# Moving the second half of a gate projection behind the last input projection block, with the attention stage's loads, value split and first maxima beside it

## The chip, the core and the metric

The kernel runs on one core of one Trainium2 chip. A core has five engines that run side by side, each through a queue of its own in a fixed order: TensorE (PE, matrix products, with weight loads shown apart as PEld), VectorE (DVE), ScalarE (ACT), GpSimd (POOL) and SyncE (SP), which here issues most of the transfers between the large memory and the core's own. The metric is device time in microseconds (us), the median of several executions.

## The reference, cut to what matters

One layer of a backbone over 2048 latent tokens and 256 context tokens, width 1024: a modulated norm, one input projection, a softmax attention group and a gated delta-rule group side by side, an output projection, then a gated MLP.

```
q_a, k_a, v_a, qkv_d, z_d, a_f, a_b, b_f, b_b = jnp.split(h @ w_in, offs, axis=-1)
...
o_attn = block_attention(ql, jnp.concatenate([kc, kl], axis=1), jnp.concatenate([vc, vl], axis=1))
o_attn = rms_norm(o_attn.astype(h.dtype), attn_out_g)
...
qd, kd, vd = gdn_inputs(qkv_d, conv_qkv_w, True)
...
o_gdn = gated_rms(ol_f + flip(ol_b), z_d, gdn_norm_g)
lat_out = jnp.concatenate([o_attn, o_gdn], axis=-1) @ w_out
```

`z_d` is the gate: 512 columns of the input projection, put through SiLU and multiplied into the delta rule's normalised output. The attention has 8 query heads on 2 key heads of 64 columns, over 18 chunks of 128 keys (2 of context, 16 latent). The delta rule has 4 heads of 128 columns and runs over the same 18 chunks in both directions.

## The kernel before, in words

Products are done with operands split into a high and a low part, so that a product is three matmuls. The kernel goes through these stages, each on all tokens:

1. `front`: modulation, first norm, keys and values of the attention (stored to `ksc`, `vsc`). The normed input stays on the core in `hl`, four chunks of 512 tokens in two parts.
2. Attention queries (stored to `qsc`), two halves of 256 columns over 16 token tiles.
3. The gate, also two halves of 256 columns over 16 token tiles (the loop over `hf` and `tt` around L950 to L972). A tile is 24 matmuls (`tokproj`, L585 to L587), SiLU on ScalarE (L963), a scaling on GpSimd (L964), a maximum on VectorE (L967, into `zmx`) and a store by SyncE (L969, to `zsc`). The second half's weights are loaded and split by `load_w` (L576, L577). `decay_setup`, a long list of small steps for the delta rule, is put into the first half at its third tile.
4. Twelve input projection blocks for the delta rule (matmuls L546 to L548, output `pg`): four each for queries, keys and values. For each block and chunk: copy out (`u`, L1076), a convolution of three steps on VectorE (`y`, L1048, L1050), SiLU (L1051), transposes on PE (`pt`, L987), scaling (`kd`, L995, L998) and a store to `gsc` (L1000). `load_g` loads and splits a block's weights. From the fifth block on, the context chunk (`hc`) comes first in each block. The second modulation's pieces (`wm`, `wacc`, `mps2`) lie between.
5. The second norm's scales (`hm` to `oscl`, L1099 to L1128): maxima over `aff2`, `mod2`, the output gain and `zmx`, spread over the partitions through two small products on PE.
6. Attention and delta rule together. Both are written as lists of planned instructions (`Plan`), which a list scheduler orders by estimated costs, buffer rings and the weights of their tracks; the order is then issued as it is. All of them show the line L422, so they are told apart by tile names. The stage begins with clearing tiles (`rows`, `qx`, `kx`, L1161 to L1164), the loads of queries, keys and values by GpSimd (`q`, `qx`, `kh`, `kx`, `vraw`), the row maxima of the first query group (`tops`: products `sm`, maxima `mx`, then `top`, `tp` and a row of `qx`), the value split (`values`: `vm`, `vst`) and the delta rule's start values (`y`, twelve copies of `i16` on ScalarE).

   In the loop over 32 groups (16 query tiles by 2 key heads), the scores `sc` of two key chunks go through the exponential to `p`, are split into `hp` and `lp`, and are multiplied with the values into `ops`; the next group's maxima run between. The delta rule has 18 steps in each direction; each loads `tT`, `tk` and `rows`, inverts a triangular matrix (`py`, `pa`, `y`, `t`) and advances a state.
7. Output projection, second norm, MLP (`po`, `ua`, `ub`, `uc`, `pdn`).

Outside the planned stages the framework's own scheduler orders instructions by the place in the program and by estimated readiness; a later instruction may be put ahead of an earlier one that waits. On-chip room is taken from pools on a left and a right stack; a tile waits until the tiles that had its room are done with.

Of the kernel before, what the change touches and what calls it, by code (L numbers as in the profile page):

```python
# [10 lines left out]
F32 = mybir.dt.float32  # L11
# [9 lines left out]
P = 128  # L21
# [9 lines left out]
HA = 8  # L31
# [163 lines left out]
class Plan:  # L195
# [5 lines left out]
    def __init__(self, tc, *psum):  # L201
        self.tc, self.psum, self.ops, self.rings, self.open = tc, psum, [], {}, None
        self.track, self.spent, self.gate, self.patience, self.rate, self.fixed = None, {}, None, {}, 2.4, (65, 65, 0, 50, 42)
# [9 lines left out]
    def wrap(self, tile_, shape, dtype):  # L213
        return Lazy(Root(None, None, None, tile_), shape, dtype)

# [53 lines left out]
    def add(self, eng, fn, name, kw):  # L269
# [170 lines left out]
def kernel(  # L440
# [511 lines left out]

    with tc.tile_pool(name="zp", bufs=2, reuse_waits="tile") as zp_:
        for hf in range(2):
            for tt in range(NTT):
                if (hf, tt) == (0, 2):
                    decay_setup()
                n_ = f"z{hf}_{tt}"
                if (hf, tt) == (1, 10):
                    wg = load_g(0)  # L960
                ps = tokproj(direct, of_chunk(tt), ws, 256, n_)
                zt = zp_.tile([P, 256], F32, tag="zt", name=f"zt_{n_}")
                S.activation(out=zt, in_=ps[:, :256], func=AF.Silu)  # L963
                G.tensor_tensor(out=zt.rearrange("p (h d) -> p h d", d=P),  # L964
                                in0=zt.rearrange("p (h d) -> p h d", d=P),
                                in1=rows[:, R_GN:R_GN + P].unsqueeze(1).broadcast_to([P, 2, P]), op=ALU.mult)
                V.tensor_reduce(out=zmx[:, 16 * hf + tt:16 * hf + tt + 1], in_=zt, axis=AX, op=ALU.max,  # L967
                                apply_absolute_value=True)
                SY.dma_start(out=zsc[tt, :, 256 * hf:256 * hf + 256], in_=zt)  # L969
            if hf == 0:  # L970
                ws = load_w(direct, wiz[1], "z1")
    pq.close()  # L972


    with ExitStack() as pg:
        hcp = pg.enter_context(tc.tile_pool(name="hcp", bufs=1, side="right", reuse_waits="tile"))
        hc = hcp.tile([P, 2, KT, TC], F32R, name="hc")
# [87 lines left out]
        for blk in range(NG):  # L1065
            ws = wg if blk == 0 else load_g(blk)
            if blk == 2:
                SY.dma_start(out=hc.bitcast(F32), in_=hcd)
# [1381 lines left out]
```

## Time and profile before

| | us |
|---|---|
| median of 3 runs | 3199.56 (3194.95 to 3201.15) |
| the profiled execution | 3198.06 |
| its span, first to last instruction | 3196.3 |
| PE busy in the span | 3053.4 (96%) |
| VectorE, ScalarE, GpSimd busy | 2385.7, 1769.9, 1531.0 |

Stages by the trace: gate matmuls from 271.2 to 370.8 (the second half from 324.5), input projection blocks from 370.8 to 712.4, attention and delta rule from about 726 to 1740, then the rest. A row of the profile gives an engine's busy time, the number of instructions, and what ended the idle time before them; matmuls overlap each other, so a matmul's own duration is longer than the distance to the next one. PEclk is the share of full clock that PE was granted.

### The profile page before, as it was taken

To read this page: it belongs to the slowest core of one execution; us is meant where nothing else is said; L and a number is where in the kernel's file an instruction comes from. 1 tells how busy PE (TensorE), PEld (TensorE's weight loads), DVE (VectorE), ACT (ScalarE), POOL (GpSimd) and SP (SyncE) were. 2 spreads that over 40 slices of the span, in tenths; PEclk is the share of its full clock that TensorE was granted. 3 is DMA by queue.
4 is the path that set the end of the run, shared out by engine and by line. 5 is a ranking of instruction groups with operands and counts; after the bars stand their busy time and mean duration, and the time that the engine had idled before them with its cause. 6 is when DMAs were issued, how large, how long until landed. Compare 5 with 4: busy or idle time off the path is not lost.

```text
span 3196.3 us, 62950 instructions
## 1 busy us (share of the span) xinstructions
PE 3053.4 (96%) x25298; PEld 1958.4 (61%) x25298; DVE 2385.7 (75%) x3669; ACT 1769.9 (55%) x2876; POOL 1531.0 (48%) x1241
## 2 busy tenths in 40 slices
PE   6889999997999999999998999999999999999998
PEld 3789978874667777777776454444444444444445
DVE  4766487887777777788885779877777777976676
ACT  4534134345777777776776546545555455544332
POOL 4786365555887776776777434323332223000000
PEclk8899999997999999999998899999999999999999
DMA  6222334663112222233332575322222222696696
GB/s 245 82 79 83 112 120 125 174 172 94 46 41 75 67 82 87 87 117 109 102 104 100 205 258 193 125 93 99 96 98 97 94 98 77 204 311 204 218 308 221
DMA packets 287333, 423.63 MB, mean 133 GB/s; under 512 B 22984, under 2 KB 166952, under 8 KB 285744
## 3 DMA queue, kind: packets, MB, share of 16 engines
q1 hardware_dynamic: 285088, 414.19, 39.2%
q0 software_dynamic: 1952, 5.42, 0.6%
q8 instruction: 198, 3.24, 0.4%
q14 instruction: 95, 0.78, 0.1%
HBM read 284.15 MB, written 135.81 MB: 131 GB/s over the span
## 4 chain that ended last, share of the span: by engine, by line
PE 76%; DVE 9%; POOL 6%; DMA 3%; issue 3%; ACT 3%; SPq 0%; POOLq 0%; DVEq 0%; ACTq 0%
PE pdn L422 12%; PE ub L422 10%; PE sc L422 7%; PE uc L422 7%; PE ua L422 6%; PE ops L422 6%; PE po L422 6%; PE sm L422 3%; PE pa L422 2%; PE pg L547 1%; PE pg L546 1%; PE pg L548 1%; PE pw L422 1%; DVE mx L422 1%; PE pm L422 1%
## 5 line engine op out<-in xcount | busy, mean ns | idle before, releaser
L422 POOL TENSOR_TENSOR lp<-p,hp 128x1024 f16<-128x1024 f32 x288 | 620.0, 2160 | 208.5 <-DVE hp L422 83.4
L422 PEld LDWEIGHTS <-ws_u 128*128 128x128 f16 x3696 | 360.7, 98 | 434.3 <-issue 9.1
L422 DVE TENSOR_REDUCE mx<-sm 128x2 f32<-128x1024 f32 (+1 forms) x320 | 356.3, 1113 | 94.7 <-PE sm L422 91.5
L422 PE MATMUL pdn<-hid,wd 128*128 128x512 f16 (+1 forms) x1980 | 400.8, 365 | 0.0
L422 ACT ACTIVATE p<-sc 128x1024 f32<-128x1024 f32 x288 | 295.2, 1025 | 127.5 <-PE sc L422 123.8
L422 PEld LDWEIGHTS <-wd 128*128 128x128 f16 x1980 | 193.8, 98 | 204.7
L422 DVE SCALAR_TENSOR_TENSOR cv<-xa,ufw,cv 128x1025 f32<-128x1025 f32 (+1 forms) x176 | 251.3, 1480 | 49.9 <-ACT cv L422 49.8
L422 POOL TENSOR_TENSOR ws_u<-raw_u,ws_u 128x512 f16<-128x512 f32 x110 | 174.4, 1597 | 139.8 <-ACT ws_u L422 120.5
L422 PE MATMUL sc<-q,kh 128*128 128x512 f16 x576 | 220.6, 383 | 6.3 <-ACT p L422 5.9
L422 PE MATMUL sc<-qx,kx 128*128 128x512 f16 x576 | 220.4, 383 | 0.0
L422 POOL TENSOR_TENSOR nrc_f<-nrc_f,mhalf 128x8 f32<-128x8 f32 x3 | 5.5, 1837 | 423.7 <-DVE nrc_f L422 423.7
L422 ACT CAST hp<-p 128x1024 f16<-128x1024 f32 x192 | 201.0, 1047 | 3.7
L422 PE MATMUL ops<-vst,hp 128*128 128x65 f16 (+1 forms) x4608 | 192.3, 194 | 1.3 <-ACT hp L422 1.1
L422 PE MATMUL ua<-blk_a,ws_u 128*128 128x512 f16 x792 | 181.4, 379 | 0.0
L422 PEld LDWEIGHTS <-hp 128*128 128x128 f16 x4608 | 165.3, 98 | 21.0 <-issue 6.9
L422 PE MATMUL po<-ol,ws_o 128*128 128x512 f16 x768 | 175.0, 385 | 0.1
L546 PE MATMUL pg<-hl,ws_g 128*128 128x512 f32 x384 | 152.8, 398 | 0.0
L422 POOL TENSOR_TENSOR usg<-usg,mhalf 128x3 f32<-128x3 f32 x22 | 20.5, 933 | 276.1 <-DVE usg L422 276.1
L548 PE MATMUL pg<-hl,ws_g 128*128 128x512 f32 x384 | 152.3, 397 | 0.0
L547 PE MATMUL pg<-hl,ws_g 128*128 128x512 f32 x384 | 151.7, 395 | 0.0
L422 ACT CAST t<-pa 128x512 f16<-128x512 f32 x216 | 124.6, 583 | 43.1 <-PE pa L422 39.3
L422 PE MATMUL sm<-kh,q 64*128 64x512 f16 (+1 forms) x320 | 118.8, 371 | 18.4 <-DVE mx L422 18.1
(704 smaller groups left out, 7787.0 us busy)
## 6 DMA issues: line engine op xcount, KB each, us to landing
rd<-in_wd SPq DMA_DIRECT2D x70, 512.0 KB
hid<-hidc SPq DMA_DIRECT2D x70, 512.0 KB
raw_u<-in_wu SPq DMA_DIRECT2D x44, 512.0 KB
tk<-gsc SPq DMA_DIRECT2D x34, 512.0 KB
tT<-gsc SPq DMA_DIRECT2D x66, 256.0 KB
hidc<-cv SPq DMA_DIRECT2D x22, 768.0 KB
wm<-in_wm SPq DMA_DIRECT2D x64, 256.0 KB
gsc<-kd SPq DMA_DIRECT2D x64, 256.0 KB
```

Source lines behind the costliest of these rows:

```text
L422: fn(**{k: v.get() if isinstance(v, Lazy) else v for k, v in kw.items()})
L546: PE.matmul(out=ps, lhsT=hi_l(k), rhs=hi_r(k), start=st, stop=False)
L547: PE.matmul(out=ps, lhsT=hi_l(k), rhs=lo_r(k), start=False, stop=False)
L548: PE.matmul(out=ps, lhsT=lo_l(k), rhs=hi_r(k), start=False, stop=en)
```

## The change

The second half of the gate projection no longer follows the first. Its weights are loaded within the last block into tiles that held the context input (`hc` becomes four tiles of a ring, `zw` follows in it, and the attention's `p` tiles after that), split by ScalarE and GpSimd. Its 16 tiles run behind the last block, and between them, at the tiles named in `todo`, stand the attention stage's loads and clearings (`loads`, tile 0), the value split (`values`, tile 4) and the row maxima of the first two query groups (`first_tops`, tiles 6 and 10), now outside the plan, with single-bank products and one maximum for each. The value split multiplies by the scale while it converts and subtracts. The attention's planned part starts with the scores; the maxima of groups 0 and 1 are dropped from it. The second norm's scales become planned instructions behind the plan's instruction at which the ninth group begins, on a track of low weight. The delta rule's start values are copied by VectorE outside the plan, its first loads are issued by SyncE as all others are, without waiting for the keys' issue, and the buffer `at` is claimed one instruction earlier.

```
+    def claim(self, t):
+
+        r, o = t.root, self.ops[-1]
+        o.allocs.append(r)
+        r.turn, r.first = r.ring.made.get(o.track, 0), o.idx
+        r.ring.made[o.track] = r.turn + 1
+        r.ops.add(o.idx)
...
+        if self.after is not None:
+            op.behind.add(self.after)
...
+    def gate_tile(hf, tt, ws, pool, shape, tag):
+        n_ = f"z{hf}_{tt}"
+        ps = tokproj(direct, of_chunk(tt), ws, 256, n_)
+        zt = pool.tile(shape, F32, tag=tag, name=f"zt_{n_}", bufs=2)[:, 0:256]
+        S.activation(out=zt, in_=ps[:, :256], func=AF.Silu)
...
+        SY.dma_start(out=zsc[tt, :, 256 * hf:256 * hf + 256], in_=zt)
...
-        for hf in range(2):
-            for tt in range(NTT):
...
-            if hf == 0:
-                ws = load_w(direct, wiz[1], "z1")
+        for tt in range(NTT):
+            if tt == 2:
+                decay_setup()
+            if tt == 10:
+                wg = load_g(0)
+            gate_tile(0, tt, ws, zp_, [P, 256], "zt")
...
+                if (blk, c) == (NG - 1, 0):
+                    zw = []
+                    for i, t in enumerate(four_tiles("zw")):
+                        raw = rp.tile([P, 2, 256], F32, tag="raw", name=f"raw_z1{i}", bufs=3)
+                        SY.dma_start(out=raw, in_=wiz[1][:, 2 * i:2 * i + 2, :])
+                        S.copy(out=t[:, 0], in_=raw)
+                        G.tensor_tensor(out=t[:, 1], in0=raw, in1=t[:, 0].bitcast(F32), op=ALU.subtract)
+                        zw += [t[:, :, 0, :], t[:, :, 1, :]]
...
+    def loads():
+        for a in range(0, NCK, 6):
+            s = ksc[a:a + 6].rearrange("c p f t -> p c f t")
+            G.dma_start(out=kh_t[0:64, a:a + 6], in_=s[0:64])
+            G.dma_start(out=kh_t[64:128, a:a + 6], in_=s[0:64])
+        G.dma_start(out=vraw, in_=vsc.rearrange("c p x -> p c x"))
+        G.dma_start(out=q0_t, in_=qsc[0])
+        G.dma_start(out=qx_t[0][64:128], in_=qsc[0][0:64])
+        for t in qx_t:
+            G.memset(t[0:64], 0.0)
+        G.memset(kx_t[0:64], ROWV)
...
+    def values():
...
+        for g in range(KV):
+            x = vraw[:, :, g * HD:(g + 1) * HD]
+            S.activation(out=vst_t[:, :, g, 0:HD], in_=x, func=AF.Copy, scale=vi[:, g:g + 1])
+            V.scalar_tensor_tensor(out=vst_t[:, :, g, HD + 1:2 * HD + 1], in0=x, scalar=vi[:, g:g + 1],
+                                   in1=vst_t[:, :, g, 0:HD], op0=ALU.mult, op1=ALU.subtract)
...
+    def first_tops(g):
...
+        for h in range(0, GR, 2):
+            for j in range(5):
...
+                sm = [pst.tile([P, 512], F32, tag="pb", name=f"sm{g}_{h}_{j}_{i}") for i in range(2)]
...
+                for i in range(2):
+                    V.tensor_reduce(out=mx[:, h + i, j:j + 1], in_=sm[i][:, 0:w], axis=AX, op=ALU.max)
...
+    todo = {0: loads, 4: values, 6: lambda: first_tops(0), 10: lambda: first_tops(1)}
+    for tt in range(NTT):
+        if tt in todo:
+            todo[tt]()
+        gate_tile(1, tt, zw, ak, [P, 512], "oacc")
+    p1.close()
...
+    for d in range(2):
+        G.memset(rows_t[d], 0.0)
+        for t in ys_t[d]:
+            V.tensor_copy(out=t, in_=i16)
...
-        for _ in tops(0, 0, *q_now):
-            pass
-        values()
...
+            if n == 8:
+                marks.append(len(plan.ops) - 1)
...
-                pr = plan.tile(ap, [P, 2, 512], F32, "p", f"p_{nm}_{c0}", RINGS["p"])
+                pr = plan.tile(hcp, [P, 2, 512], F32, "hc", f"p_{nm}_{c0}", 4)
...
-            q = SY if step else G
-            plan.gate = None if step else loaded[0]
+            q = SY
...
+    plan.track, plan.after = "m", marks[0]
+    second_scales(plan)
+    plan.after = None
```

`second_scales` holds the same instructions as stage 5 above, written for the plan; `gate_tile` holds those of stage 3.

More of the change, by code (lines that the diff above doesn't have):

```diff
@@ new lines @@
+    ak = pa.enter_context(tc.tile_pool(name="ak", bufs=1, side="right", reuse_waits="tile"))
+    VW, GR = 130, HA // KV
+    kh_t = ak.tile([P, NCK, KV, P], F16, name="kh")
+    vraw = ak.tile([P, NCK, KV * HD], F32, name="vraw")
+    vst_t = ak.tile([P, NCK, KV, VW], F16, name="vst")
+    q0_t = ak.tile([P, HA, P], F16, name="q0")
+    qx_t = [ak.tile([P, HA, P], F16, name=f"qx{i}") for i in range(2)]
+    kx_t = ak.tile([P, NCK, KV, P], F16, name="kx")
+    shift_t = ak.tile([P, 1], F32, name="shift")
@@ L1133 @@
+    vtop_t = ak.tile([P, KV], F32, name="vtop")
     pc = ExitStack()
@@ new lines @@
+    todo = {0: loads, 4: values, 6: lambda: first_tops(0), 10: lambda: first_tops(1)}
[4 more added lines that the diff above has]
+    p1.close()
+    p2 = ExitStack()
+    gy = p2.enter_context(tc.tile_pool(name="gy", bufs=1, reuse_waits="tile"))
+    rows_t = [gy.tile([P, HG, 3, P], BF16, name=f"rows{d}") for d in range(2)]
+    ys_t = [[gy.tile([P, 512], F16, name=f"y{d}{l}") for l in range(1, 7)] for d in range(2)]
@@ L1188, in load_q @@
             qx = qxs[qb % 2]
[L1189 to L1191 removed]
+            SY.dma_start(out=qt, in_=qsc[qb])
+            SY.dma_start(out=qx[64:128], in_=qsc[qb][0:64])
             return qt, qx
[L1195 to L1201 removed]
@@ L1202, in attention @@
-        loaded.append(len(plan.ops) - 1)
-        for a in range(0, NCK, 6):
-            G.dma_start(out=kx[64:128, a:a + 6], in_=ksc[a:a + 6].rearrange("c p f t -> p c f t")[64:128])
-        shift = plan.tile(ak, [P, 1], F32, "shift", "shift", 1)
-        V.scalar_tensor_tensor(out=shift, in0=gm[:, 0:1], scalar=9.0 * SC / 1024, in1=gm[:, 1:2], op0=ALU.mult, op1=ALU.mult)
-        V.tensor_scalar(out=shift, in0=shift, scalar1=PSLACK * SC, scalar2=-1.0 / ROWV, op0=ALU.min, op1=ALU.mult)
-        V.tensor_scalar(out=shift, in0=shift, scalar1=PSHIFT * SC / ROWV, scalar2=None, op0=ALU.add)
@@ L1242, in tops @@
+        q_now = plan.wrap(q0_t, [P, HA, P], F16), qxs[0]
+        kh, kx = (plan.wrap(t, [P, NCK, KV, P], F16) for t in (kh_t, kx_t))
+        shift = plan.wrap(shift_t, [P, 1], F32)
+        vst = plan.wrap(vst_t, [P, NCK, KV, VW], F16)
+        vtop = plan.wrap(vtop_t, [P, KV], F32)
         def tops(qb, g, qt, qx):
@@ L1353, in delta @@
         s0 = None
-        ys = [None]
-        for l in range(1, 7):
-            y = plan.tile(gh, [P, 512], F16, f"y{d}{l}", f"y{d}{l}", 1)
-            S.copy(out=y, in_=i16)
-            ys.append(y)
+        ys = [None] + [plan.wrap(t, [P, 512], F16) for t in ys_t[d]]
         lvm = [None] + [lv16[:, P + 64 * (6 * d + l):P + 64 * (6 * d + l + 1)].bitcast(U16) for l in range(6)]
@@ L1382, in delta @@
             q.dma_start(out=rws[0:12], in_=rsc[d, ck].rearrange("h r s t -> r h (s t)"))
-            plan.gate = None
             if lat and not first:
@@ L1503, in delta @@
                 at = f32t("at")
+                plan.claim(at)
                 S.activation(out=at, in_=pd2, func=AF.Exp)
```

211 lines of the change are left out of this document (101 added, 110 removed).

## The prediction

> **What bounds the kernel now.** I read the page's slices first, for the stretches in which TensorE (PE) is not full, and then a table by stretches for the one that the change touches.
>
> ```profile
> span 3196.3 us, 62950 instructions
> ...
> PE   6889999997999999999998999999999999999998
> ...
> PEclk8899999997999999999998899999999999999999
> ```
>
> A slice is 79.9 us. PE stands at 9 tenths nearly everywhere: it sets the pace. The tenth slice (719 to 799 us) is the exception in the middle: 7 tenths busy, and the clock granted to PE is 7 tenths too. That is the seam between the last input projection block and the attention stage.
>
> ```profile
> core 0: us, PE busy (x) PEld busy (x) DVE busy (x) ACT busy (x) POOL busy (x), PEclk, DMA share, GB/s
> 326.00:371.00 45.00, 45.00 (x383) 44.97 (x382) 11.17 (x38) 6.33 (x17) 14.88 (x16) 1.00 0.22 73
> 371.00:712.60 341.60, 333.54 (x1741) 278.60 (x1740) 271.41 (x383) 133.14 (x335) 186.93 (x240) 1.00 0.49 148
> 712.60:726.40 13.80, 3.45 (x16) 2.46 (x14) 6.49 (x10) 11.81 (x30) 11.51 (x15) 0.64 0.99 246
> 726.40:743.40 17.00, 4.63 (x17) 0.90 (x17) 12.76 (x20) 0.83 (x1) 6.84 (x6) 0.50 0.87 271
> 743.40:753.40 10.00, 7.61 (x41) 4.82 (x39) 7.78 (x11) 2.95 (x5) 1.15 (x1) 0.67 0.34 112
> 753.40:768.40 15.00, 12.51 (x92) 6.45 (x90) 13.09 (x16) 8.83 (x10) 8.39 (x4) 0.53 0.01 2
> 768.40:1720.00 951.60, 934.91 (x13737) 692.22 (x13735) 752.58 (x1100) 724.52 (x958) 713.76 (x376) 1.00 0.25 79
> ```
>
> The rows are: second half of the gate projection, input projection blocks, four pieces of the seam, and the attention stage with the delta rule beside it. In the two stages around the seam PE is busy 98% at clock 1.00. In the seam (712.6 to 768.4, 55.8 us) it is busy 28.2 us, at about half clock. In full-clock work that is 3.45 x 0.64 + 4.63 x 0.50 + 7.61 x 0.67 + 12.51 x 0.53 = 16.3 us. So **the seam loses 55.8 - 16.3 = 39.5 us of PE time.** The chain of waits shows through whom:
>
> ```profile
> 714.37 4.77 ACT y L422 x9
> ...
> 727.32 3.02 DVE reach L1118
> ...
> 765.52 2.95 PE ops L422 x64
> ```
>
> ScalarE (ACT) copies the delta rule's start values while the last convolution waits for it; VectorE (DVE) then works through the second norm's scales, the maxima of the first query group and the value split; only at 765.5 does the first product with the values run. Meanwhile nothing independent is left for PE.
>
> **The change, part by part.** *Moved: the second half of the gate projection.* Its matmuls:
>
> ```profile
> L585 PE MATMUL pq_z<-ws_z,hl x128: 277/281/366, 324.5 to 370.6; 128*128 128x256 f32 x128
> ...
> L587 PE MATMUL pq_z<-ws_z,hl x128: 276/281/366, 324.8 to 370.8; 128*128 128x256 f32 x128
> ```
>
> 384 matmuls from 324.5 to 370.8: 46.3 us, at clock 1.00. They are not removed. Before the blocks they filled time that PE would have filled anyway, so the blocks start and end about 46.3 us earlier; behind the blocks they fill the seam. What can be won is the seam's 39.5 us, less what the new order loses elsewhere. Three such losses follow.
>
> *In front.* VectorE's 11.17 us beside the moved half are 16 maxima of the gate at 0.42 us (row below), 6.7 us, which move along; the other 4.4 us finish the decay set-up and now land beside the first blocks.
>
> ```profile
> 390.00:410.00 20.00, 19.84 (x100) 16.05 (x99) 17.24 (x25) 8.28 (x18) 14.41 (x18) 1.00 0.35 117
> ```
>
> There VectorE has 2.8 us free in 20, so some of it delays PE: 0 to 4.4 us, and I take 2, the middle. The new weight split (4 loads, 4 copies on ScalarE, 4 subtractions on GpSimd, POOL) lies beside the last block, where the block row shows ACT at 39% and POOL at 55%; it replaces 8 copies and 8 VectorE subtractions. I cost it at nothing; without that cover the subtractions would hold up the first gate tile.
>
> *The new stage.* On PE it holds the 46.3 us, the last convolution's 12 transposes, the two groups of first maxima and a few small steps. Maxima and loads, from the stage before:
>
> ```profile
> 776.89 0.39 PE L422 MATMUL sm<-kh,qx 64*128 64x512 f16 x1
> 777.21 0.42 PE L422 MATMUL ops<-vst,lp 128*128 128x65 f16 x8
> L967 DVE TENSOR_REDUCE zmx<-zt_z x32: 402/419/421, 281.8 to 372.4; 128x1 f32<-128x256 f32 x32
> L422 DVE TENSOR_REDUCE mx<-sm 128x2 f32<-128x512 f32 x62 | 42.7, 689 | 15.4 <-PE sm L422 14.7
> L422 DVE TENSOR_REDUCE vm<-vraw x2: 1340/1340/1341, 742.8 to 745.1; 128x1 f32<-128x1152 f32 x2
> L422 DVE TENSOR_TENSOR vst<-vraw,vst x2: 1347/1802/2258, 761.7 to 763.9; 128x1152 f16<-128x1152 f32 x2
> L1000 SPq DMA_DIRECT2D gsc<-kd x8: 359/370/5398, 711.7 to 726.0; - x8
> 716.40 3.94 POOL L422 DMA_DIRECT2D kh<-ksc  x6
> kh<-ksc POOLq DMA_DIRECT2D x6, 192.0 KB, 7.6
> vraw<-vsc POOLq DMA_DIRECT2D x1, 1152.0 KB, 10.6
> ```
>
> A pair of maximum products takes 0.32 us of PE (776.89 to 777.21), so the 20 pairs take at most 6.4; with transposes and small steps, some 2.5 us by my estimate, the stage is about 55 us of PE. VectorE's list: rest of the convolution 6.5 (the first seam row), 16 gate maxima 6.7, two value maxima 2.7, value split 2 x 1.8 = 3.6, first maxima 2 x (16 x 0.69 + 4 x 0.42) = 25.4, copies about 2: 47 us, inside 55 if it can start. It starts with the keys. Their loads (6 issues on POOL, 3.94 us, landing 7.6 us later) write where the convolution's buffers may have lain; the last of those leaves with the transfer issued at 726.0, 13.4 us after the last block. Early case: keys at 12 us, then 35 us of VectorE work, at 47, nothing lost. Late case: keys at 13.4 + 4 + 7.6 = 25 us, done at 60, 5 over; if the values (10.6 us) come behind them too, 71, 16 over. Bounds 0 and 16; I take 4, nearest to the keys' row. Behind a waiting load on POOL stand the gate tiles' scalings, behind those ScalarE's next tile (two buffers) and then PE; that is how a late load would reach PE. SyncE (SP) is passed by the gate's 16 stores and then the delta rule's first loads, which no longer stand on POOL: they should need only the room of the first two chunks' inputs, free by half the stage, so I cost them at nothing; if they come late, attention alone starts, which the seam below prices.
>
> *The new seam.* Attention then starts with maxima and values ready. The nearest row is the last seam piece: 15.00 us, 12.51 busy: 2.5 us idle and 12.51 x 0.47 = 5.9 us given to the low clock. On entry the clock should now be 1.00, since PE comes out of 55 us of matmuls. ScalarE also switches from the gate's function to the exponential, until now in idle time:
>
> ```profile
> 725.95 1.28 ACT L422 ACT_TABLE_LOAD   x1
> ```
>
> Bounds 0 and 2.5 + 5.9 + 1.3 = 9.7; I take 2.5 + 1.3, about 4. The Trainium skill's page "ScalarE: Activation LUTs" (What ACT_TABLE_LOAD costs) adds a drain, about 2.66 us per switch: by it the seam would take 5.4 and the time would be 1.4 us longer; the trace gives the load alone.
>
> *Costed at nothing:* the second norm's scales, now some 25 small instructions behind the attention's ninth group, beside VectorE at 752.58 of 951.6 us (up to 3 if they hold a buffer that PE wants); one GpSimd memset of 3.93 us less; start values copied by VectorE instead of ScalarE; the earlier claim of one buffer in the delta rule. The last changes the planned order: -5 to +5, by the stage's whole PE idle time, 951.60 - 934.91 = 16.7 us, of which a third.
>
> **Sum**, against the profiled execution's 3198.06 us (span 3196.3 and 1.8 around it): -39.5 + 2 + 4 + 4 = -29.5, so 3168.6. The median of the runs shown, 3199.56, lies 1.5 above that execution: **3170**.
>
> **Rivals.**
>
> *Late VectorE (0.18).* Loads come late and VectorE, not PE, ends the new stage. For it: 35 us of VectorE work hang on the keys, and 0.69 us a piece is longer than PE needs for it. Against: the maxima are spread between gate tiles. Losses 4 + 14 + 6 = 24, gain 15.5: 3184. GpSimd's memsets push the same way:
>
> ```profile
> 709.37 2.12 POOL L1163 MEMSET qx<- 64x1024 f16 x2
> 711.44 3.93 POOL L1163 MEMSET kx<- 64x4608 f16 x1
> 726.37 3.93 POOL L1164 MEMSET kx<- 1x4608 f16 x1
> 726.96 0.15 DVE L1110 TENSOR_SCALAR hinv<-hinv 128x1 f32<-128x1 f32 x1
> ```
>
> The chain's 3.02 us step of VectorE ends with the memset of 726.37; small steps of its kind take 0.15. The new stage has such memsets of 3.93 and 2.1 us beside VectorE: up to 6 of the 14 us. The Trainium skill, "SBUF — State Buffer" (SBUF: two separate sides), says that VectorE and GpSimd share a port pair as an exclusive lock held for a whole instruction; the trace agrees here.
>
> *Fuller than I think (0.15).* All three losses near nothing, and the planned order a little denser: gain 39.5 + 5: 3155, give or take 5. For it: beside the 46.3 us PE had no idle time at all.
>
> *It doesn't do what it says (0.05).* The waits keep the loads behind the gate tiles, and the attention's start stays as serial as now: only the last convolution is covered. A gain of 4 or so, 3196.
>
> *Slower (0.07).* The attention stage's order is planned ahead and each engine keeps to it. If the delta rule now lags what the plan supposes, because its first loads queue on SP, PE waits at every one of its 36 steps (18 in each direction). The gain is gone at 29.5 / 36 = 0.8 us a step, that is with 46 us of PE idle time in the stage instead of 16.7; at 1.3 us a step it costs 47, and the time is 3217. Against: the same kind of plan now leaves 0.5 us a step.
>
> **How the numbers follow.** The forecast with its neighbours (3161 to 3180) gets 0.55, the rivals as given. Adding all low and all high ends gives 39.5 + 5 = 44.5 and 39.5 - 4.4 - 16 - 9.7 - 3 - 5 = 1.4 us of gain, 3155 to 3198. The range, 3153 to 3192, leaves out 0.03 below and some 0.15 above (no change, slower, the worst of late VectorE). What can be told from no change is about 0.2%, 6.4 us: forecast, late VectorE and fuller are faster (0.88), the case of no effect is the same (0.05), slower 0.07.
>
> **What would show it.** Right: blocks begin near 326 and end near 668; then some 55 us with PE at 9 tenths and clock 1.00, gate matmuls mixed with first maxima; the first score product within a few us of the last gate matmul; a tenth slice without the dip. The first loss shows as PE idle time before 500, the second as gate matmuls that wait for ScalarE or the maxima for VectorE, the third as clock below 1.00 at the attention's start. Wrong: the clock at 0.50 for over 10 us again, first maxima ending well behind the last gate matmul, or over 30 us of PE idle time inside the attention stage.

## The result: 0.6% slower

| | before | after |
|---|---|---|
| median, us | 3199.92 (3194.95 to 3201.15, 4 runs) | 3219.32 (3217.01 to 3221.38, 4 runs) |
| ratio | | 1.0063 [1.0046, 1.0081] |
| profiled execution, us | 3198.06 | 3221.38 |

The forecast was 3170. The page of the changed kernel:

```profile
span 3219.5 us, 62992 instructions
...
PE   7789899988999999999997899999999999999998
...
PEclk8899899989999999999999899999999999999999
```

A slice is 80.5 us. The tenth slice has 8 tenths where it had 7, but the fifth (322 to 402 us, the first block) and the ninth (644 to 724) have fallen to 8, and the 22nd and 23rd (1690 to 1851), where the attention gives way to the output projection, have 7 and 8 where 8 and 9 stood. The table by stretches answers to the one of before: blocks, the new stage in six pieces, the way to the first score, the attention's start, and the attention stage as a whole (columns as before).

```profile
core 0: us, PE busy (x) PEld busy (x) DVE busy (x) ACT busy (x) POOL busy (x), PEclk, DMA share, GB/s
324.00:681.40 357.40, 339.00 (x1750) 281.84 (x1749) 269.91 (x396) 135.24 (x339) 188.22 (x240) 0.98 0.50 149
681.40:690.00 8.60, 8.60 (x75) 8.56 (x74) 4.34 (x7) 4.30 (x12) 7.78 (x11) 1.00 0.78 215
690.00:700.00 10.00, 1.47 (x13) 1.26 (x11) 0.31 (x3) 1.30 (x5) 0.45 (x1) 0.73 0.81 262
700.00:710.00 10.00, 8.92 (x53) 8.18 (x54) 4.32 (x10) 0.50 (x2) 7.34 (x6) 0.75 0.37 87
710.00:722.00 12.00, 10.31 (x46) 6.66 (x46) 10.59 (x22) 3.83 (x6) 4.19 (x4) 0.72 0.10 34
722.00:740.00 18.00, 18.00 (x128) 14.99 (x127) 7.20 (x15) 1.92 (x5) 3.40 (x5) 1.00 0.12 37
740.00:758.30 18.30, 18.30 (x128) 15.16 (x127) 8.22 (x16) 2.22 (x5) 5.50 (x7) 1.00 0.16 47
758.30:768.10 9.80, 4.51 (x15) 1.19 (x14) 8.74 (x23) 0.38 (x1) 1.06 (x2) 0.74 0.81 283
768.10:783.10 15.00, 13.60 (x122) 7.47 (x120) 5.95 (x7) 9.49 (x10) 7.39 (x4) 0.72 0.06 18
768.10:1753.00 984.90, 959.31 (x14034) 707.66 (x14032) 761.52 (x1123) 747.55 (x982) 738.14 (x386) 1.00 0.24 78
```

The blocks take 15.7 us longer than before. The gate tiles behind them run at full rate only from 722. Then 9.9 us pass between the last gate matmul (758.2) and the first score (768.1). Set against the forecast's own terms, in the profiled execution:

| | forecast | measured | miss |
|---|---|---|---|
| first block matmul at | 324.6 | 324.0 | -0.6 |
| first to last block matmul | 341.6 + 2 | 357.3 | +13.7 |
| last block matmul to first score | 55 + 4 | 86.8 | +27.8 |
| entry: 15 us less PE busy x clock | 4 | 15 - 13.60 x 0.72 = 5.2 | +1.2 |
| first score to last product with values, less the entry | 981.0 as before (989.4 - 8.4) | 990.8 - 5.2 = 985.6 | +4.6 |
| last product with values to first output product | 21.7 as before | 28.2 | +6.5 |

They add up to 53.2 us; the whole miss is 3221.38 - 3168.6 = 52.8. So the cause is in three places: **the first block, the new stage and the last seam**. Each got experiments of its own. Four kernels with the same program up to the blocks started them at 321.6, 324.0, 325.0 and 327.5, so stages are compared by their length, not by the clock time at which they end. The lengths scatter too, since each comes from one profiled execution: these four blocks took 361.3, 357.3, 361.5 and 361.6 us, while their new stages took 86.5 to 87.3. In the kernels of which no edit aims at the last seam that seam took 27.0 to 28.2, so 5.3 to 6.5 us of it are the change's; from the first score to the last product with values the kernels with the changed plan took 988.1 to 991.3 (e8, below, 995.3), beside 989.4 before.

### The profile page after: what moved, and what is told of

Read it like the earlier page. It is cut to its first block, busy times and chain, and to the rows that moved or that the text cites. A ratio compares the mean times of both kernels' runs of the same rounds, so it can differ in the third digit from the quotient of the medians.

```text
span 3219.5 us, 62992 instructions
## 1 busy us (share of the span) xinstructions
PE 3061.1 (95%) x25298; PEld 1958.0 (61%) x25298; DVE 2379.3 (74%) x3691; ACT 1764.9 (55%) x2860; POOL 1531.6 (48%) x1238
## 4 chain that ended last, share of the span: by engine, by line
PE 75%; DVE 10%; POOL 6%; DMA 3%; ACT 3%; issue 3%; SPq 0%; POOLq 0%; DVEq 0%; ACTq 0%
PE pdn L432 12%; PE ub L432 10%; PE uc L432 7%; PE sc L432 7%; PE ua L432 6%; PE po L432 6%; PE ops L432 6%; PE sm L432 2%; PE pa L432 1%; PE pg L557 1%; PE pg L558 1%; PE pg L556 1%; DVE mx L432 1%; PE pw L432 1%; DVE y L1064 1%
## 5 line engine op out<-in xcount | busy, mean ns | idle before, releaser
L432 DVE TENSOR_REDUCE mx<-sm 128x2 f32<-128x1024 f32 x300 | 334.2, 1114 | 100.1 <-PE sm L432 96.4
L432 ACT CAST hid<-hid 128x1024 f16<-128x1024 f32 x84 | 81.0, 971 | 94.8 <-DVE hid L432 50.0
```

The lines of the kernel that those rows point to most:

```text
L432: fn(**{k: v.get() if isinstance(v, Lazy) else v for k, v in kw.items()})
```

## The experiments

### The first block (15.7 us)

The groups of instructions of the changed kernel from 322 to 372 us (busy, mean ns, then idle time before them and what ended it):

```profile
L1052 DVE TENSOR_REDUCE wacc<-wm 128x128 f32<-128x512 f32 x10 | 10.2, 1040 | 7.5 <-DMA rsc<-rt 4.6 <-POOL wm L1050 2.8
...
L1001 PE MATMUL pt<-k,y 128*128 128x128 f32 x12 | 2.8, 380 | 4.0 <-ACT y L1065 3.9
...
L1055 PEld LDWEIGHTS mps<-k,wacc 128*128 128x128 f32 x8 | 1.7, 256 | 8.2 <-DVE wacc L1054 8.2
```

VectorE waits for `rsc<-rt`, the store of the decay set-up's last tile, before it may write `wacc`; PE waits for `wacc` and for the first convolution `y`. In the built program's layout `rt` (bytes 184480 to 193696 of a partition) lies under `y` (184224 to 190368) and `wacc` (to 191392). Before, the store went out at 343.4, and the moved half of the gate stood between it and the first `wacc` (369.8) and `y` (382.0); now it goes out at 342.0, and they come at 346.5 and 348.4. Six kernels take the parts of this away:

```
e1:  rt = [dp.tile([n4, 6, 3, P], BF16, tag="rt", ..., bufs=2) for i in range(2)]   # rt in two halves, two stores
e5:  pool tp laid out before up                        # other tiles of the block lie over rt
e9:  e5, and pad = tp.tile([P, 640], F32, name="pad", bufs=1)      # y and wacc no longer over rt
e12: if mods and not 4 <= blk < 8 and blk > 0:         # modulation pieces only from the second block on
e15: e9 and e12
e10: e1, e9 and e12
```

> One part of the decay set-up alone is changed against the changed kernel: each direction's tile rt is made as two tiles of half the size in a ring of two, so that the second direction need not wait for the first one's whole store. The number of VectorE steps (36 of 0.21 us), the bytes stored and their place stay. Theory (a chain of waits in front: rt's store frees the room in which the blocks' first y and wacc lie): the last store of rt is issued near 332 instead of 342.0, VectorE's first wacc comes near 336 instead of 346.5, PE busy in 344 to 364 rises from 8.3 to over 16 us, the blocks end near 671 instead of 681.3, and the time is about 10 us lower (3206 to 3213). Rival (VectorE's busy time in front is what delays the blocks, as the prediction priced it): the same work at the same place, nothing gained, 3216 to 3222.

> Against the changed kernel only the order in which two pools are laid out changes: the blocks' pool of wacc, tk, sq and kd (tp) lies first, that of u and y (up) behind it. So the first wacc, u and y no longer lie over rt of the decay set-up; their work and everybody's order are as before. Theory (a chain through rt's room, of which the half-size rt removed only 3.4 us because the last transposes of rt stand behind block matmuls on PE): VectorE's first wacc or y comes near 335 instead of 346.5, PE's busy time in 344 to 364 rises from 8.3 of 20 us to over 17, the blocks end near 671 instead of 681.3. Rival (VectorE's own busy time): VectorE starts near 335, is full to 365 and PE still loses over 8 us there; blocks end at 678 or later. Behind the blocks kd now lies under the room of q, whose load stands ahead of the gate's scalings on POOL, so a gap of some 8 us stays there under both. Theory 3209 (3205 to 3213), rival 3216 to 3221.

> The pools tp and up again in the other order, with 2.5 KB left empty between tp's last tile and u: now neither wacc nor u nor y lies over rt or over the parts bp that rt is made of (with the order alone, u still waited for bp's last transposes at 341). VectorE's built order has the first y between the steps of rt. No work changes. Theory (rooms and their chain): the first u comes at 329 to 331 instead of 334.7 and the first y right behind instead of at 348.4, PE's busy time in 344 to 364 is over 16 of 20 us (8.3 in the changed kernel), the blocks end at 669 to 674 instead of 681.3. Rival (VectorE's and the modulation pieces' own work in the first block): PE loses as much in 344 to 384 as with the order alone (12 us in full-clock work), blocks end at 677 or later. Theory 3209 (3204 to 3212); rival 3213 to 3219.

> One edit against the changed kernel: the second modulation's pieces begin with the second block instead of the first (the last four fall into the last block). The rooms are those of the changed kernel, so y and wacc still wait for rt's store at 346.5. Theory (the pieces' chain through three raw buffers: load, product on GpSimd, sum on VectorE, small product in PE's order; started 22.5 us behind the blocks' first product instead of 1 us ahead of it): that chain no longer stands between the first block's products, and the blocks take 345 to 349 us instead of 357.3, ending at 669 to 673; time 3207 to 3212. Rival (the room that y waits for): VectorE's first y still comes near 347, PE runs out of its three banks at 342 and loses 6 us or more in full-clock work there; blocks 350 to 354 us, ending at 674 to 678, 3211 to 3216.

> The changed kernel with the rooms of e9_rooms_apart (y and wacc not under rt) and the modulation pieces from the second block on as in e12_pieces_late; rt stays one tile. Theory (two delays, each enough by itself to hold PE back in the first block: y's room until rt is stored, and the chain of the pieces in PE's order; both must go): blocks 343 to 348 us instead of 357.3, total 3206 to 3212. Rival (the two half tiles in e10_front_clear did the work): blocks 352 to 356, total 3213 to 3219.

> The same, with rt in halves, and the second modulation's pieces (two loads, two products on GpSimd, two sums of 1.0 us and an addition on VectorE, one small product on PE each) beginning with the second block instead of the first; the last four then fall into the last block. If the rooms alone were the cause, this ends the blocks no more than 2 us earlier than the run with the rooms apart. If the pieces' work in the first block costs PE time too, the blocks end at 667 to 670 and over 4 us before that run's. Time 3204 to 3208.

| | first two blocks, us | all blocks, us | PE busy in 344 to 364 | median, us | ratio to before |
|---|---|---|---|---|---|
| before | 50.9 | 341.6 | | | |
| after | 66.6 | 357.3 | 8.33 | 3219.32 | 1.0063 [1.0046, 1.0081] |
| e1_halves | 62.7 | 355.0 | 11.19 | 3219.15 | 1.0063 [1.0046, 1.0079] |
| e5_swap | 63.7 | 354.6 | 11.82 | 3214.19 | 1.0039 [1.0025, 1.0053] |
| e9_rooms_apart | 66.7 | 355.3 | 8.56 | 3213.90 | 1.0040 [1.0027, 1.0054] |
| e12_pieces_late | 59.0 | 353.1 | 14.12 | 3221.05 | 1.0065 [1.0051, 1.0079] |
| e15_apart_late | 51.9 | 353.8 | 20.00 | 3216.93 | 1.0052 [1.0039, 1.0066] |
| e10_front_clear | 49.3 | 345.0 | 20.00 | 3207.13 | 1.0017 [1.0008, 1.0026] |

The first column runs from the first block matmul to the first of the third block. It holds the whole loss of the changed kernel, 15.7 us (three others with the same program up to there took 67.9 to 69.9). The first four expected a gain of 6 us or more from one part and all missed. What is left over says why. With the rooms apart (e9), from 322 to 372 us, the first `y` comes at 332.7 instead of 348.4, and PE waits all the same, for the pieces:

```profile
L1056 PEld LDWEIGHTS mps<-k,wacc 128*128 128x128 f32 x6 | 1.6, 326 | 6.6 <-DVE wacc L1055 6.6
```

With the pieces gone from this block but the room as it was (e12, same stretch), `y` waits for the store and PE for `y`:

```profile
L1001 PE MATMUL pt<-k,y 128*128 128x128 f32 x16 | 3.0, 316 | 5.9 <-ACT y L1065 5.9
...
L1062 DVE TENSOR_SCALAR y<-u,cols 128x512 f32<-128x512 f32 x5 | 2.4, 481 | 3.4 <-DMA rsc<-rt 3.4
```

With both gone, PE is full in that stretch (the table in 20 us steps from 324 to 504, one row and the sum, of e15 and then of e10):

```profile
344.00:364.00 20.00, 20.00 (x94) 16.45 (x93) 11.34 (x19) 5.96 (x13) 6.10 (x8) 1.00 0.26 83
...
sum 180.00, PE 170.18 PEld 142.35 DVE 121.07 ACT 64.18 POOL 90.25; mean PE 18.91 PEld 15.82 DVE 13.45 ACT 7.13 POOL 10.03
```

```profile
344.00:364.00 20.00, 20.00 (x101) 16.64 (x101) 11.14 (x18) 6.14 (x14) 9.01 (x14) 1.00 0.21 66
...
sum 180.00, PE 174.95 PEld 145.41 DVE 125.03 ACT 66.76 POOL 93.41; mean PE 19.44 PEld 16.16 DVE 13.89 ACT 7.42 POOL 10.38
```

So **two chains held PE in the first two blocks**: with the rooms apart alone nothing comes back of the 15.7 us, with the pieces gone alone 7.6, with both 14.7. VectorE's busy time alone was not it: in 344 to 364, e9 has VectorE busy for 14.18 us of 20 and PE for 8.56. The 20.00 us of PE in e15 and e10 show less, since the pieces that they move are VectorE's work too.

By its two forecasts, though, e15 came out as its rival said (blocks 352 to 356, time 3213 to 3219): behind the second block it loses most of the gain again, and only the halves of `rt` keep it. Up to 460 us PE waits 5.5 us for `tk` and 4.2 for split weights. A room is part of it once more. In the layout of e9 and e15, `y` and `wacc` have left `rt`, but `sq`, which a block's `tk` is made from and which lay clear of `rt` before, lies over it now. ScalarE's `sq` from 322 to 372 us, in e9 and then in e10:

```profile
L1022 ACT ACTIVATE sq<-pt 128x512 f32<-128x512 f32 x4 | 2.4, 596 | 6.8 <-PE pt L1002 4.7 <-DMA rsc<-rt 1.3 <-DVE ss L1024 0.8
```

```profile
L1024 ACT ACTIVATE sq<-pt 128x512 f32<-128x512 f32 x5 | 3.0, 599 | 2.1 <-PE pt L1004 2.1
```

In e15, as in e9, the set-up's last store goes out late, at 349.9, and the first `sq`, at 354.4, waits for it; the first `tk` comes 39.8 us behind the first block matmul. In e10, with the halves, the store goes out at 338.0, `sq` does not wait for it, and `tk` comes 25.2 us behind. How much of the 8.8 us between e15 and e10 this is, no run separates.

Putting the pieces off probably has a price of its own: the last four now reach behind the blocks, and the way from there to the first score takes 91.4 us in e12, 88.6 in e15 and 92.8 in e10, where it was 86.8.

### The new stage (86.8 us instead of 59)

In the changed kernel ScalarE's first two tiles of the moved half come only at 699.84, and they waited for a store of the last convolution (timeline of ScalarE, 690 to 702 us); PE, three tiles ahead, stopped for them (waits of PE, 681 to 775: total, times, longest):

```profile
690.24 1.15 ACT L1009 ACTIVATE kd<-pt,beta 128x128 f32<-128x128 f32 x4 [1.05 <-DVE kd L1012]
699.84 0.66 ACT L967 ACTIVATE zt_z<-pq_z 128x256 f32<-128x256 f32 x2 [8.46 <-DMA gsc<-kd]
```

```profile
PE pq_z L595 <- ACT zt_z L967: 9.0, 2, 8.8
PE sm L1202 <- DVE mx L1205: 6.5, 11, 1.7
```

The first line has two causes that could be told apart: the tiles `zt` have the room in which the blocks' `kd` lay, or, as the prediction had it, a load on GpSimd holds up the tiles' scaling. The second line is VectorE: the first maxima keep two banks busy (a bank is one of the buffers that PE writes to), one reduction for each.

```
e2: gate_tile(1, tt, zw, c2, [P, 256], "zt")           # zt where no kd lay (after: ak, [P, 512], "oacc")
e3: todo = {..., 8: loads_kx}                          # clearing and loading of kx, kb and er moved to tile 8
e4: e2 and e3
e6: sm = pst.tile([P, 2, 512], F32, tag="pb", ...)     # a pair of products in one two-bank tile, one maximum
    todo = {0: loads, 3: values, 4: first_tops(0), 6: first_tops(1)}
```

> The second half's gate tiles zt lie in another pool, 256 columns wide, over the blocks' weights instead of over the last convolution's kd; all else as in the changed kernel. Theory A (what PE waits for at 691 is the room of zt, free only when kd's last stores have landed): ScalarE's first zt comes near 685 instead of 699.8 and PE's 8.8 us gap at 691.5 is gone. Theory B (the prediction's: kx's clearing waits on POOL and the gate's scalings stand behind it): the first zt comes early too, but ScalarE's third waits for POOL's first scaling at 706, so that PE, three tiles further with its three banks, stands still from about 697 to 707; the gap moves and stays 9 to 10 us. Both have a cost: the built order now puts the first maximum product behind gate tile 7 instead of 4, and 15 products instead of 9 behind the last gate matmul, some 6 x 0.69 = 4 us more at the seam, 2.5 less between. A: 3219 - 9 + 1.5 = 3211; B: 3220.

> The clearing and the loads of kx, and the loads and copies behind them (kb, er, lv, n, i), stand before gate tile 8 instead of tile 0; zt lies where it lay in the changed kernel. Theory A (room of zt): ScalarE's first zt stays at 699.8 and PE's gap at 691.5 stays 8 to 9 us; only POOL's first scaling comes earlier, near 700.5 instead of 706.3, worth 0 to 4 us. Theory B (kx on POOL): the gap at 691.5 is gone, worth 9. 18 products instead of 9 stand behind the last gate matmul, 9 x 0.69 = 6 more at the seam, 3.7 less between. A: 3218 to 3222; B: 3212.

> Both edits: zt in the other room, and kx with what follows it before gate tile 8. By A with B behind it, PE runs from 681.5 through the gate tiles without a gap over 1.5 us before 710, at clock 1.00; that stretch (681.5 to 722) gains 9 us of gap and about 6 us that the lower clock took, and the seam gives back some 2.5: 3219 - 12 = 3207 (3203 to 3212). If something else is late (the keys' landing, VectorE), a gap of over 5 us stands elsewhere before 722 and the time stays within 3215 to 3222.

> The first maxima alone: a pair of products goes into one tile of two banks with one maximum for both (the form of the kernel before), in a ring of two, and the value split and the two groups stand at gate tiles 3, 4 and 6 instead of 4, 6 and 10. Theory (single products between gate matmuls cost PE 0.41 us more each, and 9 of 40 are left behind the last gate matmul): the gap at 691 stays; from 700 on PE needs 13 gate tiles x 2.82 + 20 pairs x 0.4 + 2, that is 47 us with some 4 of waiting, and no maxima stand behind the last gate matmul; first score product near 753 instead of 768.1, time 3204 (3201 to 3208). Rival (VectorE sets the pace of this stretch): 20 maxima of 1.33 us, 13 of 0.42 and the value split take it 42 us or more without a break, the last maximum comes behind the last gate matmul, first score product not before 760, 3211 or more.

| | last gate matmul | first score | last block matmul to first score | median, us | ratio to before |
|---|---|---|---|---|---|
| after | 758.2 | 768.1 | 86.8 | 3219.32 | 1.0063 [1.0046, 1.0081] |
| e2_gate_room | 746.5 | 759.4 | 78.3 | 3212.95 | 1.0048 [1.0032, 1.0063] |
| e3_keys_late | 749.5 | 764.2 | 82.7 | 3220.25 | 1.0062 [1.0047, 1.0077] |
| e4_both | 744.2 | 759.0 | 77.6 | 3211.20 | 1.0041 [1.0026, 1.0056] |
| e6_two_banks | 757.4 | 758.2 | 74.7 | 3210.18 | 1.0031 [1.0021, 1.0041] |

With `zt` in another room the long wait is gone and PE is full where it had stood still (e2):

```profile
690.00:700.00 10.00, 10.00 (x88) 10.00 (x87) 1.42 (x8) 2.30 (x7) 8.25 (x13) 1.00 0.93 249
```

In e3 the same wait stands (8.6 us in one piece); what it gains of the stage, 4 us, comes later. So **it was the room, not the load on GpSimd.** The gate matmuls end 11.7 us earlier in e2, the first score comes only 8.7 earlier: 15 products for the maxima instead of 9 are now left behind the last gate matmul. With both edits (e4) the stage is hardly shorter than with the room alone. e6 leaves none there: its first score follows 0.8 us behind the last gate matmul instead of 9.9. It changes two things, though, the form of the products and the tiles at which they stand, and no run separates the two. It landed between its two forecasts, because VectorE now sets the pace before that (e6):

```profile
710.00:722.00 12.00, 7.77 (x33) 4.81 (x33) 12.00 (x18) 2.94 (x4) 3.70 (x2) 0.57 0.03 10
```

### All at once, and one group only

e8 joins e5, e2 and e6, moves `kx` to tile 8 and the value split and both groups to tiles 2, 3 and 4, loads the keys and values ahead of the clearings into rooms laid out in the order of their loads, and lets ScalarE make the start values' copies. e11 joins e10, e2 and e6, has e8's order of rooms, loads by SyncE, clears and loads `kx` at tile 12, leaves the copies to VectorE, and keeps only group 0's maxima between the gate tiles, while group 1's go back into the plan:

```
todo = {0: loads, 2: values, 4: lambda: first_tops(0), 12: loads_kx}
...
ahead = tops(*groups[n + 1], ...) if n < len(groups) - 1 else iter(())
```

> The changed kernel with all four causes taken out except the last seam's: tp laid out ahead of up; zt in the room of the block weights; in the attention's pool the order kh, vraw, q, qx, vst, kx, so that what is loaded first lies over nothing that the last convolution still uses, and kx with what follows it before gate tile 8; pairs of maxima in two banks; the start values copied by ScalarE instead of VectorE. If the causes add up as measured singly: blocks end near 671, the gate stage takes 45 + 8 + 4 = 57 us, first score product near 733 to 737 (753.5 in the kernel before, 768.1 in the changed one), and with the last seam's 6.5 us still lost 3198 - 18 + 6.5 = 3186 (3180 to 3192), under the kernel before. If VectorE is the bound of the new stage, it ends at 745 or later and the time is 3195 or more.

> All causes taken out that the runs have named, with VectorE's share of the new stage halved: front as in the run before this; zt over the block weights; the attention pool's order kh, vraw, q, qx, vst, kx; loads of the stage issued by SyncE; kx before gate tile 12; the first group's maxima in pairs of two banks at gate tile 4; the second group's maxima back in the plan, beside the first group's scores; the start values copied by VectorE. Theory: the new stage's length is the landing of the keys plus VectorE's work behind it (41 us from 704 to 745 with both groups); with one group PE is the bound, 16 x 2.82 + 10 x 0.4 + some 4 us: 53 us from the blocks' end near 669, first score product at 722 to 730, attention stage 4 us longer, last seam still 27 us: 3198 + (726 - 753.5) + 4 + 5.5 = 3180 (3174 to 3188). If something else bounds the stage, the first score product stands behind 738 and the time is over 3190.

e8 measured 3201.69, ratio 1.0004 [0.9995, 1.0013]. Its first score comes at 745.8, 66.6 us behind the last block matmul, but the first exponential much later (e8, timeline of ScalarE):

```profile
744.47 6.32 ACT L1235 COPY y<-i 128x512 f16<-128x512 f16 x12
750.69 0.68 ACT L1217 ACTIVATE qx<-tp,shift 1x512 f16<-1x512 f32 x1
751.38 1.28 ACT L432 ACT_TABLE_LOAD   x1
752.68 1.02 ACT L432 ACTIVATE p<-sc 128x1024 f32<-128x1024 f32 x1
```

Twelve copies that nothing needed yet stood ahead of the first exponential in ScalarE's queue, with the second group's row of `qx` behind them, and PE waited 6.9 us for it instead of 1.4. That and the last seam (27.2 us against 21.7 before) cost more than the score, 7.7 us earlier than before, had won. The blocks, 355.4 us, had kept most of their loss, so e8 missed its 3186. e11 measured 3194.29, ratio 0.9975 [0.9964, 0.9986]: **faster than the kernel before**, with 344.7 us of blocks (322.9 to 667.6) and the first score 63.4 us behind them. Its expectation of 3180 still missed: the first score came at 731.0 instead of 726, attention stage and last seam kept 7.2 and 6.0 us where 4 and 5.5 were allowed for, and the profiled execution, 3189.73, lies 4.6 below the median.

### The last seam (6.5 us)

SyncE's issues around the end of the attention (start, duration, what), first of the kernel before, then of the changed one:

```profile
1702.58 21.84 SPq L422 DMA_DIRECT2D osm<-fin  x2
1724.52 0.37 SPq L422 DMA_DIRECT2D oraw<-oat  x1
...
1743.93 0.32 SPq L422 DMA_DIRECT2D oat<-oacc  x1
```

```profile
1721.40 23.60 SPq L432 DMA_DIRECT2D osm<-fin  x2
1759.91 0.32 SPq L432 DMA_DIRECT2D oat<-oacc  x1
1760.33 0.37 SPq L432 DMA_DIRECT2D oraw<-oat  x1
```

Before, the first two output tiles were loaded 17 to 19 us ahead of the attention's last store; now all of them come behind it. The first theory was room: with `p` gone to another ring, `oraw` lies over `hp` and `lp`, which are used to the end, where before it lay over tiles of the delta rule.

```
e7:  before, with pool ap on the left                  # puts hp and lp under oraw, as after has it
e13: after, with the pools ap and gf in each other's place   # oraw over gf, done with at about 1744
e18: (G if qb == NTT - 1 else SY).dma_start(out=oat[qb], in_=oacc)    # the last store on GpSimd's queue
e16: e13 and e18
e14: e11 and e13
e17: e14 and e18
```

> The kernel before, with one pool moved: ap (p, hp, lp of the attention) lies on the left between the delta rule's pools, so that the output projection's first oraw tiles lie over p, hp and lp as they do over hp and lp in the changed kernel, instead of over the delta rule's tiles. Theory (the 6.5 us that the changed kernel loses between attention and output projection come from this room): the first oraw load, at 1724.5 in the kernel before, waits for the last use of p or hp, some 15 to 18 us, and the stretch from the last ops product to the first po product grows from 21.7 to about 28 us; all ahead of it is the same; time 3199.5 + 6 = 3205.5 (3203 to 3208). Rival (the later delta rule or the order of the plan, not the room, does it): the stretch stays at 21 to 23, 3198 to 3201.

> The changed kernel, with the attention's split tiles hp and lp and the delta rule's gf tiles swapped in their places on the chip, so that the first output tiles' loads oraw lie over gf, which is done with at about 1744, and no longer over hp and lp, which are used until the last product with the values. Theory (the last seam grew because of the room of oraw): first oraw load issued 10 to 25 us ahead of the last product with the values, last seam 21 to 23 us instead of 28.2, total 3212 to 3215. Rival (as in the kernel before, where the same wait was put in and the total stayed): the seam shrinks, but the attention stage grows by as much, total 3217 to 3221. If the wait is not of the room, the seam stays at 27 to 29.

> The changed kernel with the last attention tile's store issued by GpSimd and nothing else: the loads stand first in SyncE's queue but their room still lies under the attention's split tiles hp and lp. Theory (queue and room must both go): the first oraw load waits for the room until about 1757, seam 26 to 28, total 3217 to 3220. Rival (the queue alone was the cause): seam 21 to 25, total 3213 to 3216.

> The kernel e13_last_room with the last attention tile's store issued by GpSimd instead of SyncE, so that the output tiles' loads no longer stand behind it in SyncE's queue. Theory (two things hold those loads back, the queue and the room, and both must go): first oraw load at about 1745, beside the last attention group, first output products with weights 21 to 25 us behind the last product with the values (26.9 to 28.2 before), total 3 to 6 us below e13_last_room, 3218 to 3221. Rival (the chain of loads is not what the seam waits for): seam 27 or more, total 3222 to 3225.

> The kernel e11_one_group with the same swap of rooms as e13_last_room. Theory: last seam 21 to 23 us instead of 27.7, total 3187 to 3190, ratio to before 0.996. Rival (attention stage grows by as much): 3193 to 3196.

> The kernel e14_both_ends with the last attention tile's store issued by GpSimd. Theory: first oraw load at about 1703, last seam 21 to 24 us instead of 27.4, total 3184 to 3187, ratio to before 0.995 to 0.996. Rival: no change, 3189 to 3192.

| | first oraw load | last product with values to first output product | median, us | ratio to before |
|---|---|---|---|---|
| before | 1724.5 | 21.7 | | |
| e7_room_before | 1739.0 | 27.2 | 3199.62 | 0.9997 [0.9988, 1.0006] |
| after | 1760.3 | 28.2 | 3219.32 | 1.0063 [1.0046, 1.0081] |
| e13_last_room | 1763.3 | 27.5 | 3223.78 | 1.0073 [1.0061, 1.0085] |
| e18_queue_only | 1766.1 | 27.0 | 3221.89 | 1.0066 [1.0049, 1.0083] |
| e16_queue_room | 1746.1 | 23.5 | 3216.14 | 1.0049 [1.0033, 1.0064] |
| e14_both_ends | 1732.7 | 27.4 | 3190.25 | 0.9970 [0.9959, 0.9981] |
| e17_best | 1700.8 | 23.5 | 3187.30 | 0.9960 [0.9947, 0.9972] |

e7 showed that the room can do it: the seam grew by 5.5 us in the kernel before. But e13 refuted it as the whole cause: with another room the loads still come behind the store, because SyncE takes its queue in order (e13):

```profile
1762.88 0.32 SPq L432 DMA_DIRECT2D oat<-oacc  x1
1763.31 0.37 SPq L432 DMA_DIRECT2D oraw<-oat  x1
```

With the queue clear and the room not, SyncE waits for the last products that use it (e18, waits of SyncE, 1720 to 1800):

```profile
SPq L432 <- PE ops L432: 12.6, 1, 12.6
```

Only with both gone do the loads come early, beside the attention (e17), and the seam shrinks by 4 us, in e16 as in e17:

```profile
1700.82 0.37 SPq L432 DMA_DIRECT2D oraw<-oat  x1
```

As in the first block, two waits held the same work. What the seam cost in time shows in e16 against e13 (7.6 us less by the medians, 4.0 of it in the seam) and in e17 against e14 (3.0 less, 3.9 in the seam). The seam stays 1.8 us longer than before. In e7 the total did not move although the seam grew, since that edit's first score came 2.3 us earlier and its attention stage was shorter. Why the build puts the store ahead of the loads after the change and behind them before was not found.

e17_best is the version to keep: 3187.3 (3185.69 to 3188.74, 5 runs), 12 us below the kernel before. Its stretches from the last block matmul on:

```profile
669.20:700.00 30.80, 27.49 (x217) 25.08 (x216) 20.90 (x34) 8.61 (x26) 14.29 (x14) 1.00 0.83 206
700.00:710.00 10.00, 6.74 (x55) 6.33 (x56) 7.29 (x11) 1.77 (x5) 2.87 (x4) 1.00 0.33 98
710.00:722.00 12.00, 12.00 (x91) 10.30 (x91) 9.50 (x13) 3.57 (x6) 2.75 (x4) 1.00 0.10 33
722.00:729.90 7.90, 7.90 (x70) 7.79 (x68) 2.16 (x4) 1.45 (x3) 3.27 (x5) 1.00 0.16 52
729.90:745.00 15.10, 12.11 (x119) 6.45 (x118) 11.88 (x21) 9.90 (x11) 9.74 (x6) 0.89 0.61 199
```

The seam runs at clock 1.00 up to the first score.

## Why the prediction was wrong

**What held.** The blocks moved forward as said (324.0, forecast 324.6). The weight split cost nothing: the first gate matmul follows the last block matmul by 0.2 us. And the idea itself pays once the hindrances are gone: in e17 the blocks take 343.8 us (forecast 343.6) and the first score comes 61.6 us behind them (59), though that stage holds one group's maxima and not the two of the forecast.

**What came near by luck.** The entry into the attention cost 5.2 us, forecast 4. But the forecast had the clock at 1.00 there; it was 0.72, which cost 13.60 x 0.28 = 3.8 us, and PE was idle for 1.4 us where 2.5 and a table load were put. The table load is there, 1.28 us from 769.08, with 0.02 us ahead of it and the exponential 0.01 us behind it, so no drain shows beside it.

**The step "In front" failed.** It weighed busy time: VectorE has 2.8 us free in 20, so 0 to 4.4 us. What delayed PE was no mere lack of VectorE time but two chains, through the room of `rt` and through the pieces' place in PE's order (e9, e12, e15). The moved half had covered both; the prediction asked of the weight split what its cover was, and did not ask it of the moved half itself. It cost 15.7 us, over three times the upper bound.

**The step "The new stage" had its main wait in the wrong place and the products for the maxima too cheap.** VectorE's list was sized about right, 44 us busy where 47 were listed. For the wait it named GpSimd's loads; it was a room from which `kd` still had to be stored (e2 against e3). By PE busy x clock, the stretch from 690 to 722 lost (10 - 1.47 x 0.73) + (10 - 8.92 x 0.75) + (12 - 10.31 x 0.72) = 16.8 us where 4 were forecast. The products for the maxima were sized by a pair that runs together, 0.32 us. Alone between gate matmuls they cost more: from 722 to 758.3 PE was full with 232 gate matmuls (0.1206 us each by the 46.3 us for 384) and 18 single products with four transposes, so these took 36.3 - 28.0 = 8.3 us, by this estimate over 0.4 each instead of 0.16.

**The step "The new seam" priced the entry and left out what stands ahead of it**: 9.9 us in which VectorE's reductions, two banks at a time, let the last nine products out one by one, with the start values' copies between. This is the rival *late VectorE*, in part: its 14 us were meant for late keys, and here the keys, issued from 682.2 to 685.6, landed within 6.3 us. Pairs at earlier tiles took these 9 us away (e6); which of the two did it is not shown.

**No step dealt with the last seam**: 6.5 us, of which 4 went when both the order in SyncE's queue and the room that the move of `p` had changed were taken away (e13, e18, e16).

**The rivals.** *Slower* had the sign, not the mechanism: from first to last score PE is idle for 984.90 - 959.31 = 25.6 us, not 46; in the kernel before, over a stretch as long:

```profile
753.50:1737.00 983.50, 960.93 (x14028) 708.28 (x14027) 769.49 (x1120) 746.65 (x986) 735.05 (x385) 0.99 0.25 78
```

That is 22.6 us, so a lag of the delta rule as priced there is not in the trace. *It doesn't do what it says* fell as well: loads and values come beside the gate tiles. *Fuller than I think* fell with the steps above.

**What stays open.** In e17 the first score to the last product with values takes 998.7 us instead of 989.4. Group 1's maxima are back in that stage, but no run separates them. Nor does a run show what is left of the loss in the blocks of e10 and e17, 3.4 and 2.2 us.

## What to carry to other kernels

Before independent work is moved out of a stretch, look at what it covered there: which tiles get the room of the work ahead of it, and when that is stored. Where two waits hold the same engine, taking either one away may show little; take away both before a theory is dropped. And look at what a moved tile now lies over: apart from one tile, `rt` held up the next. An engine with free time can still be late, so price a step by its chain of waits, and look at the order of the queues in the built program wherever a pool or a ring has changed.

## What the hardware showed

- The clock fell not only after PE stood still, but also while it was busy two thirds of the time. After the 8.8 us wait at 691 the changed kernel's PE works at 0.50 until about 705 and is at full clock by 706. From 708 single products wait for VectorE, and 4 us later it is at 0.50 again (2 us steps):

```profile
702.00:704.00 2.00, 2.00 (x11) 2.00 (x11) 0.98 (x1) 0.00 (x0) 2.00 (x1) 0.50 0.00 0
...
706.00:708.00 2.00, 2.00 (x20) 2.00 (x18) 0.00 (x0) 0.00 (x0) 1.70 (x3) 1.00 0.94 221
...
710.00:712.00 2.00, 1.39 (x5) 0.54 (x5) 2.00 (x6) 0.00 (x0) 0.00 (x0) 0.94 0.01 3
712.00:714.00 2.00, 1.53 (x3) 0.30 (x3) 2.00 (x7) 1.16 (x2) 0.00 (x0) 0.50 0.00 0
...
720.00:722.00 2.00, 2.00 (x12) 1.41 (x13) 1.32 (x3) 0.39 (x1) 1.22 (x2) 1.00 0.20 66
```

  From 710 to 716 PE has 3 to 5 instructions a step, where a full step holds 11 to 20: by its busy share it works, and its longest pause from 708 to 716 is 0.58 us, but that did not keep the clock up. From 700 to 722 the clock alone cost 8.92 x 0.25 + 10.31 x 0.28 = 5.1 us. In e2, without the wait, the clock from 690 to 700 was 1.00.
- VectorE's reductions were not slowed by a GpSimd memset. The two maxima of the values ran wholly within one (the tile `vm`, shortest, median and longest in ns and first and last start; then GpSimd's timeline; both of the changed kernel):

```profile
L1172 DVE TENSOR_REDUCE vm<-vraw x2: 1342/1342/1343, 700.4 to 701.6; 128x1 f32<-128x1152 f32 x2
```

```profile
700.36 3.94 POOL L1155 MEMSET kx<- 64x4608 f16 x1 [9.90 <-DVE shift L1168]
```

  The prediction's rival had put up to 6 us on such a collision. The Trainium skill, "SBUF — State Buffer" (Who interferes with whom), says that a reduction on this chip never contends with GpSimd; the trace agrees: 1342 ns beside the memset, and 1340 in the kernel before, where GpSimd did nothing beside them.
